# Feed-forward passes over one column tile: 1024 inner channels at a time instead of 512

## The chip, the core and the metric

The kernel runs on one core of a Trainium2 chip. Five engines of the core work side by side and meet through semaphores: TensorE (PE in the profile, its weight loads PEld), VectorE (DVE), ScalarE (ACT), GpSimd (POOL) and SyncE (SP), which here issues nearly all DMAs. The metric is the device time of one execution, in microseconds (us). One profiled execution gives the trace; its times are the ones quoted, counted from the start of the span.

## The reference

Two layers of a streaming encoder are run for 1024 prompt frames and 32 sample frames that share all weights, in float32. Layer 0 mixes with a spatial gating unit, layer 1 with a pooling mixer; each is followed by the feed-forward network (FFN) that the change is about. Cut to that part:

```python
D_MODEL = 1024; D_FF = 4 * D_MODEL
for i in range(2):
    mod = silu(c) @ w_ada[i] + b_ada[i]              # 6 conditioning vectors of 1024
    sh1, sc1, gt1, sh2, sc2, gt2 = split(mod, 6)
    ...                                              # mixer, residual with gt1
    h = rmsnorm(x, g_norm[i, 2]) * (1 + sc2) + sh2
    f = square(relu(h @ ffn_w_up[i])) @ ffn_w_down[i]
    x = x + gt2 * rmsnorm(f, g_norm[i, 3])
```

`c` is one vector per group, so the prompt frames share one set of conditioning vectors and the sample frames another. The matrices are 1024 by 4096 up and 4096 by 1024 down.

## The kernel before

**Layout.** Activations lie transposed: 128 channels on the partitions, frames along the free axis, 8 blocks of 128 channels (`KB`). The 1056 frames form three column tiles (`TILES`): 384, 384, and 256 prompt + 32 sample frames = 288. `acc[t]` holds a tile's accumulator, `hh[t]` and `hl[t]` the normalised input as a high and a low part. Every float32 product is made of three matmuls in the rounded format `F32R` (`products`, lines 1024 to 1026 of the profile): high weight by high input, high by low, low by high.

**Weights.** A weight piece of 512 KB is loaded into one of three staging buffers (`raw`, `RAW_SLOTS`), copied to its high part by ScalarE (line 528) and subtracted to its low part by VectorE (`wl`). High and low part take two of 16 slots (`w_tile`); four slots are lent out and called back once the FFN starts (`LEND_AT`, `w_call`), so the FFN holds at most six pieces. `stream` is the one list in which all pieces are loaded, with pieces of `w_ada` between them (`some_ada`); the latter are multiplied and summed on VectorE (`aa`, four instructions a piece, a fold after every fourth).

**FFN passes.** `passes` lists the FFN's work in order: (layer, 512-channel block, tiles). For one tile, `ffn_item` makes four up products of 24 matmuls (`up(j)`; ScalarE applies relu, square and the high copy `fh`, VectorE the low part `fl`) and puts the down products into `pending`. They are issued by `flush()` behind the first up product of the next pass, so the last `fl` has that long to get ready. `down()` makes eight products of 12 matmuls (`pg`), each with an addition to `acc` on VectorE (`accumulate`; the first block is a copy on ScalarE). For the first two tiles together, `pair_item` needs seven block products where two tiles would need eight, from input combinations made by `combos()`; its down products follow at once. The hidden parts live in five places each (`t_hid`); the pair borrows staging tiles for three more.

**Order.** The program is written out by Python. `fillers` are generators with the vector work between matrix products: `ffn0_t` (after the gating mixer: residual, norm, modulation, which `ffn0`'s first pass on tile t needs), `ffn1_t` (residual of layer 0's FFN, pooling mixer, residual, norm, modulation for layer 1), `out_t` (the output). `weave()` runs after every product: it takes at most one piece of the stream, and then steps of the first two fillers as long as a planner's clock for VectorE is behind its clock for TensorE. An addition is booked at 0.16 us + n/930, other operations alike; a filler may ask for a gap (`yield 1.2`), in which the second filler is served. Where a pass begins a tile, `finish()` issues the rest of its filler at once (`run_ffn`). The framework then puts each engine's instructions in its own queue; instructions that are ready can be moved ahead of others there, and `PE` mostly stays in written order.

The pair combinations use the memory of the lent slots (tag `R`); `singles` tells `combos()` that it may start.

Of the kernel before, what the change touches and what calls it, by code (L numbers as in the profile page):

```python
# [10 lines left out]
F32R = mybir.dt.float32r  # L11
# [4 lines left out]
P = 128  # L16
# [11 lines left out]
NT = len(TILES)  # L28
# [7 lines left out]
def tile_stream_encoder_step(  # L36
# [100 lines left out]
    def ps_up(name):  # L137
        return psum.tile([P, 512], F32, tag="pu", bufs=2, name=name)
# [7 lines left out]
    def t_m(name):  # L146
        return work.tile([P, 384], F32, tag="m", bufs=3, name=name)
# [4 lines left out]
    def t_hid(kind, name, dtype=F32R):  # L152
        return work.tile([P, 384], dtype, tag="h" + kind, bufs=5, name=name)
# [88 lines left out]
    def add_w(key, ap, shape, kind="w"):  # L242
        stream.append((kind, key, ap, shape))
# [21 lines left out]
    lent = {"left": LENT, "called": False}  # L265
# [18 lines left out]
    def w_free(key):  # L284
        for i in held.pop(key):
            if i >= 0 and lent["called"]:
                lent["left"] -= 1
            else:
                slots.append(i)
# [60 lines left out]
                )  # L350

    def w_chunk(n):
        l, c, tiles = passes[n]
        for j in range(4):
            f = 4 * c + j
            add_w(
                ("up", n, j),
                ffn_w_up[l][:, f * P : (f + 1) * P].rearrange("(k p) f -> p k f", p=P),
                (8, P),
                ("one", "two")[j % 2] if tiles == PAIR else "w",  # L360
            )
        for q in range(4):
            add_w(
                ("dn", n, q),
                ffn_w_down[l][c * 512 : (c + 1) * 512, q * 256 : (q + 1) * 256].rearrange(
                    "(j p) d -> p j d", p=P
                ),
                (4, 256),
            )

    every = list(range(NT))
    PAIR = every[:2]
    passes = [(0, c, [0]) for c in (0, 1, 6, 7)]
    passes += [(0, c, [1]) for c in (0, 1)]
    passes += [(0, c, PAIR) for c in range(2, 6)]
    passes += [(0, c, [1]) for c in (6, 7)]
    passes += [(0, c, [NT - 1]) for c in range(8)]
    passes += [(1, c, [t]) for t in PAIR for c in range(4)]  # L380
    passes += [(1, c, PAIR) for c in range(4, 8)]
    passes += [(1, c, [NT - 1]) for c in range(8)]
    LEND_AT = ("up", 0, 0)

    rest = []
# [1 line left out]
    def some_ada(n):  # L387
        for _ in range(min(n, len(rest))):
            add, l, j = rest.pop(0)
            add(l, j)  # L390
# [25 lines left out]
    for n in range(len(mixes)):  # L416
        w_groups(n)
        if n < 2:
            some_ada(8)
    for n, (l, c, tiles) in enumerate(passes):  # L420
        w_chunk(n)
        if tiles == PAIR:
            some_ada((6, 2)[l])
        elif l == 0 and c > 1 and len(tiles) == 1 and tiles != [NT - 1]:
            some_ada(2)
    some_ada(99)

    worder = [s[1] for s in stream if s[0] in ("w", "one", "two")]
# [236 lines left out]
    def run_deferred(force=False):  # L665
        n = len(deferred)
        while n > 0 and (force or deferred[0][0] <= time["pe"]):
            deferred.pop(0)[1]()
            n -= 1
# [31 lines left out]
    def stream_ready():  # L701
        k = state["next"]
        if k >= len(stream):
            return False
        if subs:
            return len(slots) >= subs[0][0]
        return len(slots) >= {"w": 2, "one": 3, "two": 3}.get(stream[k][0], 0)

    def stream_step():

        if not subs and stream[state["next"]][0] == "one":
            issue()
            state["next"] += 1
        k = state["next"]
        kind, key, ap, shape = stream[k]
        issue()
        run_deferred()
        if kind == "two":
            if not subs:
                quads(key[1], key[2], raws.pop(k - 1), raws.pop(k))  # L720
            subs.popleft()[1]()
            if not subs:
                state["next"] += 1
            issue()
            return
        r = raws.pop(k)
        if kind == "w":
            do_w(key, r)
        elif kind == "wide":
            do_ada(*key, r, 512)  # L730
        elif kind == "ada":
            if k < first_ada:
                do_ada_pe(*key, r)
            else:
                do_ada(*key, r, 256)
        else:
# [27 lines left out]
    def w_finish(key):  # L764
        w_free(key)
# [511 lines left out]
    pending = []  # L1277
# [43 lines left out]
    def sgu_item(p, t, mix, after):  # L1321
# [123 lines left out]
                flush()  # L1445
        pending.append(down)

    def ffn_item(p, t, after):
        l, c, tiles = passes[p]
        last = t == tiles[-1]  # L1450
        n = ncol[t]
        hid = []

        def up(j):
            ps = ps_up(f"pf{l}_{c}_{t}_{j}")
            products(ps, n, up_terms(("up", p, j), t))
            if last:
                w_finish(("up", p, j))
            r = t_m(f"r{l}_{c}_{t}_{j}")
            act(out=r[:, :n], in_=ps[:, :n], func=AF.Relu)  # L1460
            a, b = t_hid("h", f"fh{l}_{c}_{t}_{j}"), t_hid("l", f"fl{l}_{c}_{t}_{j}")
            act(out=r[:, :n], in_=r[:, :n], func=AF.Square)
            split(a, b, r, n)
            hid.append((a, b))

        def down():
            for d in range(KB):
                ps = ps_dn(f"pg{l}_{c}_{t}_{d}")
                wh, wl = need_w(("dn", p, d // 2))
                terms = []  # L1470
                for j in range(4):
                    o = j * 256 + (d % 2) * P
                    a, b = hid[j]
                    terms.append((wh[:, o : o + P], wl[:, o : o + P], a[:, :n], b[:, :n]))
                products(ps, n, terms)
                accumulate(t, d, ps, c == 0)
                if d == 0 and after is not None:
                    st = Stat(t, f"rf{l}_{t}", l == 0 or t < NT - 1)
                if after is not None:
                    st.square(d)  # L1480
                    if l == 1 and t == NT - 1:
                        scale_last(d)
                        if d < len(LAST):
                            turn_x(d)
                        if d in (2, 4, 6):
                            turn_last(d - 2)
                            turn_last(d - 1)
                if last and d % 2 == 1:
                    w_finish(("dn", p, d // 2))
                weave(d % 2)  # L1490
            if after is not None:
                after(st)

        for j in range(4):
            up(j)
            weave()
            if j == 0:
                flush()
                if l == 1 and c == 7 and last and t == NT - 1:
                    load_last()  # L1500
        pending.append(down)


    def pair_item(p, after, ends):
        l, c, tiles = passes[p]
        n = ncol[0]
        hid = {t: [None] * 4 for t in tiles}
        made = [0]
# [181 lines left out]
    singles = []  # L1690
# [208 lines left out]
        fillers.append((f"ffn1_{t}", run()))  # L1899

    def run_ffn(l, after):
        for p, (pl, c, tiles) in enumerate(passes):
            if pl != l:
                continue
            ends = [t for t in tiles if not any(q[0] == l and t in q[2] for q in passes[p + 1 :])]
            if tiles == PAIR:
                pair_item(p, after, ends)
                continue
            for t in tiles:
                if c == 0:  # L1910
                    if any(f[0] == f"ffn{l}_{t}" for f in fillers):
                        flush()
                    finish(f"ffn{l}_{t}")
                if tiles == [1] and c == 0:
                    singles.append(l)
                ffn_item(p, t, after if t in ends else None)

    run_ffn(0, to_pool)


# [154 lines left out]
```

## Time and profile before

| | us |
|---|---|
| median of 3 runs (2162.13 to 2167.15) | 2162.45 |
| the profiled execution | 2162.36 |
| its span, first to last instruction | 2160.6 |
| PE busy | 2116.0 (98%) |
| DVE busy | 1580.9 (73%) |
| ACT busy | 1050.2 (49%) |
| mean busy share of the 16 DMA engines, queue q1 | 48.2% |

The profiled execution takes 1.8 us beyond its span and lies 0.1 us under the median. Matmuls overlap, so a row gives one of 384 columns some 0.33 us while the next starts 0.17 us later; the number of matmuls that start in a stretch tells more than PE's busy time. The FFN of layer 0 runs from 613 to 1385 us, that of layer 1 from 1391 to 2151 us. Of each, the passes are: first tile alone, second tile alone, pairs, (layer 0: second tile again,) third tile.

### The profile page before, as it was taken

The numbers are of one execution on the slowest core, as the hardware profiler recorded it, in microseconds if no ns is written. First come the engines' busy times: TensorE is split into PE (matmuls) and PEld (weight loads), VectorE is DVE, ScalarE is ACT, GpSimd is POOL, SyncE is SP. The second block draws the span as 40 slices with busy tenths as digits, with TensorE's granted clock in tenths as the row PEclk, the third lists the DMA queues.
The fourth block names the chain that finished last, engine by engine and source line by source line (L and its number), as shares of the span: only waits on it lengthen the run. The fifth ranks groups of instructions, "written<-read, shape, count | busy, mean of one in ns | idle before, by whom it ended". The sixth has DMA issues, their size and how long they took to land.

```text
span 2160.6 us, 33037 instructions
## 1 busy us (share of the span) xinstructions
PE 2116.0 (98%) x12930; PEld 2045.1 (95%) x12930; DVE 1580.9 (73%) x2778; ACT 1050.2 (49%) x1801; POOL 22.3 (1%) x44
## 2 busy tenths in 40 slices
PE   8999999999999999999999999799999999999998
PEld 6878999999999999999998999799999999999998
DVE  6778837567788757788886896957969765588564
ACT  5634331233455454443455666555655443455454
POOL 0000000000000000000000000000000000001100
PEclk9999999999999999999999999899999999999999
DMA  8586524353344543333474765455544322247762
GB/s 289 167 257 209 183 76 135 99 161 114 115 135 126 162 126 99 116 117 108 138 225 137 214 201 180 135 154 164 167 139 127 108 81 85 80 129 224 176 187 82
DMA packets 401904, 320.16 MB, mean 148 GB/s; under 512 B 47406, under 2 KB 365142, under 8 KB 401748
## 3 DMA queue, kind: packets, MB, share of 16 engines
q1 hardware_dynamic: 400820, 316.77, 48.2%
q8 instruction: 101, 1.65, 0.3%
q0 software_dynamic: 896, 1.28, 0.2%
q14 instruction: 55, 0.45, 0.1%
q10 hardware_dynamic: 32, 0.01, 0.0%
HBM read 287.34 MB, written 30.66 MB: 147 GB/s over the span
## 4 chain that ended last, share of the span: by engine, by line
PE 86%; DVE 6%; DMA 3%; ACT 3%; issue 1%; DVEq 0%; SPq 0%; ACTq 0%
PE pg L1025 10%; PE pg L1026 10%; PE pg L1024 10%; PE pf L1024 7%; PE pf L1025 7%; PE pf L1026 7%; PE po L1024 3%; PE po L1025 3%; PE po L1026 3%; PE pu L1024 3%; PE pu L1026 3%; PE pu L1025 3%; DMA raw<-in_w_ada_dram 2%; PE pv L1050 2%; PE pv L1052 2%; PE pv L1051 2%
## 5 line engine op out<-in xcount | busy, mean ns | idle before, releaser
L1024 PE MATMUL pg<-fh,wh_dn 128*128 128x384 f32 (+1 forms) x1344 | 431.5, 322 | 2.4 <-ACT wh_dn L528 2.4
L1026 PE MATMUL pg<-fh,wl_dn 128*128 128x384 f32 (+1 forms) x1344 | 429.1, 319 | 0.4 <-DVE wl_dn L80 0.4
L1025 PE MATMUL pg<-fl,wh_dn 128*128 128x384 f32 (+1 forms) x1344 | 429.3, 320 | 0.2 <-DVE fl L80 0.2
L1024 PE MATMUL pf<-hh,wh_up 128*128 128x384 f32 (+1 forms) x1024 | 325.6, 319 | 11.2 <-ACT hh L984 6.5
L1025 PE MATMUL pf<-hl,wh_up 128*128 128x384 f32 (+1 forms) x1024 | 324.4, 317 | 0.0
L1026 PE MATMUL pf<-hh,wl_up 128*128 128x384 f32 (+1 forms) x1024 | 323.7, 316 | 0.3 <-DVE wl_up L80 0.2
L528 ACT ACTIVATE wh_dn<-raw 128x1024 fp32r<-128x1024 f32 x160 | 169.1, 1058 | 198.6 <-PE pg L1025 126.8
L1024 PEld LDWEIGHTS pg<-fh,wh_dn 128*128 128x128 f32 x1344 | 252.5, 188 | 4.2 <-ACT wh_dn L528 2.6
L80 DVE TENSOR_TENSOR wl_dn<-raw,wh_dn 128x1024 fp32r<-128x1024 f32 x160 | 195.7, 1224 | 83.0 <-ACT wh_dn L528 76.6
L1025 PEld LDWEIGHTS pg<-fl,wh_dn 128*128 128x128 f32 x1344 | 252.7, 188 | 1.6 <-DVE fl L80 0.7
L1026 PEld LDWEIGHTS pg<-fh,wl_dn 128*128 128x128 f32 x1344 | 252.9, 188 | 0.7 <-DVE wl_dn L80 0.7
L80 DVE TENSOR_TENSOR acc<-acc,pg 128x384 f32<-128x384 f32 (+1 forms) x336 | 173.4, 518 | 72.9 <-PE pg L1026 72.6
L80 DVE SCALAR_TENSOR_TENSOR aa<-raw,csil,aa 128x512 f32<-128x512 f32 (+1 forms) x364 | 206.7, 623 | 20.9 <-DMA raw<-in_w_ada_dram 20.9
L80 DVE TENSOR_TENSOR wl_up<-raw,wh_up 128x1024 fp32r<-128x1024 f32 x128 | 156.3, 1222 | 81.7 <-ACT wh_up L528 81.5
L1024 PEld LDWEIGHTS pf<-hh,wh_up 128*128 128x128 f32 x1024 | 193.7, 190 | 14.0 <-ACT hh L984 7.6
L528 ACT ACTIVATE wh_up<-raw 128x1024 fp32r<-128x1024 f32 x128 | 135.5, 1060 | 130.0 <-PE pf L1025 78.4
L1026 PEld LDWEIGHTS pf<-hh,wl_up 128*128 128x128 f32 x1024 | 194.3, 190 | 1.0 <-DVE wl_up L80 0.9
L1025 PEld LDWEIGHTS pf<-hl,wh_up 128*128 128x128 f32 x1024 | 194.1, 190 | 0.9 <-DVE hl L80 0.7
L80 DVE TENSOR_TENSOR fl<-r,fh 128x384 fp32r<-128x384 f32 (+1 forms) x168 | 87.0, 519 | 43.1 <-ACT fh L1284 42.0
L1024 PE MATMUL po<-ush,wh_o 128*128 128x384 f32 (+1 forms) x336 | 108.0, 321 | 0.0
L1026 PE MATMUL po<-ush,wl_o 128*128 128x384 f32 (+1 forms) x336 | 107.7, 321 | 0.0
L1025 PE MATMUL po<-usl,wh_o 128*128 128x384 f32 (+1 forms) x336 | 107.7, 320 | 0.0
(387 smaller groups left out, 4254.7 us busy)
## 6 DMA issues: line engine op xcount, KB each, us to landing
raw<-in_ffn_w_up_dram SPq DMA_DIRECT2D x160, 512.0 KB, 4.0
raw<-in_ffn_w_down_dram SPq DMA_DIRECT2D x160, 512.0 KB, 3.4
raw<-in_w_ada_dram SPq DMA_DIRECT2D x92, 512.0 KB, 4.3
raw<-in_sgu_w_in_dram SPq DMA_DIRECT2D x40, 512.0 KB, 4.0
xd<-acc SPq DMA_DIRECT2D x8, 1536.0 KB, 7.8
raw<-in_sgu_w_out_dram SPq DMA_DIRECT2D x24, 512.0 KB, 3.6
xo_r<-xd SPq DMA_DIRECT2D x32, 384.0 KB, 4.0
vd<-vt SPq DMA_DIRECT2D x32, 256.0 KB, 4.5
```

Of the source, the lines that this page charges most:

```text
L80: return op(out, *args, **kw)
L528: act(out=wh, in_=r, func=AF.Copy)
L1024: mm(ps[:, :n], wh, rh, start=i == 0, stop=False)
L1025: mm(ps[:, :n], wh, rl, start=False, stop=False)
L1026: mm(ps[:, :n], wl, rh, start=False, stop=i == last)
L1050: mm(ps[:m, :], a_h, wh[:, o : o + 512], start=k == 0, stop=False)
L1051: mm(ps[:m, :], a_h, wl[:, o : o + 512], start=False, stop=False)
L1052: mm(ps[:m, :], a_l, wh[:, o : o + 512], start=False, stop=k == KB - 1)
```

## The change

The tuple of a pass gets a fourth member m, the number of 512-channel blocks that it takes. For m = 2 there are eight up products and then eight down products of 24 matmuls, each over eight hidden blocks, with one addition to the accumulator where there were two. A down piece of the weights is then 1024 channels by 128 columns instead of 512 by 256. The down products of such a pass aren't put into `pending` but issued directly behind its last up product. Thirteen passes have m = 2: two of the first tile, one of the second and four of the third in layer 0, two and four of the first and third in layer 1. Passes of the second tile before the pairs, and the pairs, stay as they are; in layer 0 the pairs take blocks 4 to 7 instead of 2 to 5. The eight `w_ada` pieces that were spread two by two behind four single passes of layer 0 stand four by four behind the two passes of the first tile. The hidden parts of m = 2 use five more places, in memory of tag `R`; so `singles` is set later, after the first up product on the second tile.

```diff
 def w_chunk(n):
-        for j in range(4):
+        for j in range(4 * m):
...
-        for q in range(4):
+        w = 256 // m
+        for q in range(4 * m):
             add_w(
                 ("dn", n, q),
-                ffn_w_down[l][c * 512 : (c + 1) * 512, q * 256 : (q + 1) * 256].rearrange(
+                ffn_w_down[l][c * 512 : (c + m) * 512, q * w : (q + 1) * w].rearrange(
                     "(j p) d -> p j d", p=P
                 ),
-                (4, 256),
+                (4 * m, w),
...
-    passes = [(0, c, [0]) for c in (0, 1, 6, 7)]
-    passes += [(0, c, [1]) for c in (0, 1)]
-    passes += [(0, c, PAIR) for c in range(2, 6)]
-    passes += [(0, c, [1]) for c in (6, 7)]
-    passes += [(0, c, [NT - 1]) for c in range(8)]
-    passes += [(1, c, [t]) for t in PAIR for c in range(4)]
-    passes += [(1, c, PAIR) for c in range(4, 8)]
-    passes += [(1, c, [NT - 1]) for c in range(8)]
+    passes = [(0, c, [0], 2) for c in (0, 2)]
+    passes += [(0, c, [1], 1) for c in (0, 1)]
+    passes += [(0, c, PAIR, 1) for c in range(4, 8)]
+    passes += [(0, 2, [1], 2)]
+    passes += [(0, c, [NT - 1], 2) for c in (0, 2, 4, 6)]
+    passes += [(1, c, [0], 2) for c in (0, 2)]
+    passes += [(1, c, [1], 1) for c in range(4)]
+    passes += [(1, c, PAIR, 1) for c in range(4, 8)]
+    passes += [(1, c, [NT - 1], 2) for c in (0, 2, 4, 6)]
...
         if tiles == PAIR:
             some_ada((6, 2)[l])
-        elif l == 0 and c > 1 and len(tiles) == 1 and tiles != [NT - 1]:
-            some_ada(2)
+        elif l == 0 and tiles == [0]:
+            some_ada(4)
...
+    more_hid = [None, 0]
+
+    def take_hid(name, many):
+
+        if not many:
+            more_hid[:] = [None, 0]
+        else:
+            i = more_hid[1]
+            more_hid[1] += 1
+            if i % 10 >= 5:
+                if more_hid[0] is None:
+                    assert not lent["left"]
+                    more_hid[0] = work.tile([P, 5, 2, 384], F32R, tag="R", bufs=1, name="fx" + name)
+                return more_hid[0][:, i % 5, 0], more_hid[0][:, i % 5, 1]
+        return t_hid("h", "fh" + name), t_hid("l", "fl" + name)
...
 def ffn_item(p, t, after):
-            a, b = t_hid("h", f"fh{l}_{c}_{t}_{j}"), t_hid("l", f"fl{l}_{c}_{t}_{j}")
+            a, b = take_hid(f"{l}_{c}_{t}_{j}", m > 1)
...
-                wh, wl = need_w(("dn", p, d // 2))
+                wh, wl = need_w(("dn", p, d * m // 2))
                 terms = []
-                for j in range(4):
-                    o = j * 256 + (d % 2) * P
+                for j in range(4 * m):
+                    o = j * 256 // m + (d % 2) * P * (2 - m)
...
-                weave(d % 2)
+                weave((d + 1) * m % 2 == 0)
...
-        for j in range(4):
+        for j in range(4 * m):
             up(j)
             weave()
             if j == 0:
                 flush()
+                if tiles == [1] and c == 0:
+                    singles.append(l)
...
-        pending.append(down)
+        if m > 1:
+            down()
+        else:
+            pending.append(down)
```

More of the change, by code (lines that the diff above doesn't have):

```diff
@@ L352, in w_chunk @@
     def w_chunk(n):
-        l, c, tiles = passes[n]
-        for j in range(4):
+        l, c, tiles, m = passes[n]
+        for j in range(4 * m):
             f = 4 * c + j
@@ L419, in tile_stream_encoder_step @@
             some_ada(8)
-    for n, (l, c, tiles) in enumerate(passes):
+    for n, (l, c, tiles, m) in enumerate(passes):
         w_chunk(n)
@@ L1446, in sgu_item @@
         pending.append(down)
+    more_hid = [None, 0]
[11 more added lines that the diff above has]
+        return t_hid("h", "fh" + name), t_hid("l", "fl" + name)
     def ffn_item(p, t, after):
-        l, c, tiles = passes[p]
+        l, c, tiles, m = passes[p]
         last = t == tiles[-1]
@@ L1487, in down @@
                             turn_last(d - 1)
-                if last and d % 2 == 1:
-                    w_finish(("dn", p, d // 2))
-                weave(d % 2)
+                if last and (d + 1) * m % 2 == 0:
+                    w_finish(("dn", p, d * m // 2))
+                weave((d + 1) * m % 2 == 0)
             if after is not None:
                 after(st)
-        for j in range(4):
+        for j in range(4 * m):
             up(j)
@@ L1498, in ffn_item @@
                 flush()
-                if l == 1 and c == 7 and last and t == NT - 1:
+                if tiles == [1] and c == 0:
+                    singles.append(l)
+                if l == 1 and c + m == 8 and last and t == NT - 1:
                     load_last()
-        pending.append(down)
+        if m > 1:
+            down()
+        else:
+            pending.append(down)
     def pair_item(p, after, ends):
-        l, c, tiles = passes[p]
+        l, c, tiles, _ = passes[p]
         n = ncol[0]
@@ L1901, in run_ffn @@
     def run_ffn(l, after):
-        for p, (pl, c, tiles) in enumerate(passes):
+        for p, (pl, c, tiles, m) in enumerate(passes):
             if pl != l:
@@ L1913, in run_ffn @@
                     finish(f"ffn{l}_{t}")
-                if tiles == [1] and c == 0:
-                    singles.append(l)
                 ffn_item(p, t, after if t in ends else None)
```

## The prediction

> **What bounds the kernel.** I read the page first, then the table of waits for TensorE, then its busy time stretch by stretch.
>
> ```profile
> span 2160.6 us, 33037 instructions
> ...
> PE 2116.0 (98%) x12930; PEld 2045.1 (95%) x12930; DVE 1580.9 (73%) x2778; ACT 1050.2 (49%) x1801; POOL 22.3 (1%) x44
> ```
>
> TensorE is the bound, and the change takes no matmul away: two passes of 192 become one of 384. What can be won is only the time in which TensorE stands. The additions that go are VectorE's, 73% busy on average. Where does TensorE stand, and on whom?
>
> ```profile
> PE pn_r_0x L897 <- ACT sc_r_0x L882: 8.8, 1, 8.8
> PE pf L1024 <- ACT hh L984: 6.5, 2, 5.1
> ...
> PE pf L1024 <- ACT wh_up L528: 3.7, 2, 2.0
> PE pn_rf L897 <- ACT sc_rf L882: 2.7, 1, 2.7
> PE pg L1024 <- ACT wh_dn L528: 2.4, 1, 2.4
> PE pg L1025 <- DVE fx L80: 1.8, 6, 0.5
> ```
>
> Total, times, longest: a few long waits. The stretches around them, with two undisturbed ones first (core, PE busy with its count, PEld, DVE, ACT, POOL, clock, DMA):
>
> ```profile
> 1116.00:1134.00 18.00, 18.00 (x106) 18.00 (x105) 14.79 (x22) 8.24 (x12) 0.00 (x0) 1.00 0.47 139
> 2060.00:2078.00 18.00, 18.00 (x138) 18.00 (x137) 13.38 (x16) 8.77 (x12) 0.00 (x0) 1.00 0.69 204
> 1094.00:1104.00 10.00, 8.22 (x47) 7.76 (x46) 8.92 (x13) 4.58 (x8) 0.00 (x0) 1.00 1.02 298
> 1146.00:1170.00 24.00, 18.91 (x113) 17.09 (x106) 19.40 (x51) 14.79 (x35) 0.00 (x0) 0.86 0.24 70
> 1372.00:1396.00 24.00, 10.13 (x49) 8.78 (x48) 23.71 (x39) 10.33 (x18) 0.00 (x0) 0.64 0.45 143
> 2042.00:2060.00 18.00, 15.24 (x103) 14.67 (x102) 6.33 (x10) 7.80 (x13) 0.00 (x0) 0.91 0.54 153
> 2078.00:2090.00 12.00, 10.03 (x64) 9.80 (x63) 6.10 (x7) 6.43 (x12) 0.00 (x0) 0.86 0.80 230
> ```
>
> A matmul of 384 columns takes 18/106 = 0.17 us, one of 288 18/138 = 0.13. What a stretch lacks beyond its own matmuls is lost, the low clock included:
> - D, 1094 to 1104: 10 - 47 x 0.17 = 2.0 us; a weight's load is late.
> - A, 1146 to 1170, the third tile of layer 0 begins: some 28 of 384 columns and 85 of 288, so 24 - 4.8 - 11.1 = 8.1 us.
> - B, 1372 to 1396, layer 1 begins: 32 of 288 and 17 of 384, so 24 - 4.2 - 2.9 = 16.9 us. VectorE is busy for 23.7 of these 24.
> - C, 2042 to 2060 and 2078 to 2090: 18 - 103 x 0.13 = 4.6 and 12 - 64 x 0.13 = 3.7, together 8.3 us.
>
> 35.3 us in all can be won at these four places.
>
> **The change, part by part.** Additions: a double pass issues 8 where two single passes issued 16, so each of the 13 double passes saves 8, 104 in all.
>
> ```profile
> L80 DVE TENSOR_TENSOR acc<-acc,pg 128x384 f32<-128x384 f32 x224 | 123.2, 551 | 48.4 <-PE pg L1026 48.2
> L80 DVE TENSOR_TENSOR acc<-acc,pg 128x288 f32<-128x288 f32 x112 | 50.2, 451 | 24.5 <-PE pg L1026 24.4
> ```
>
> Directly they are worth nothing: they run beside 12 other matmuls. They count where VectorE's queue of filler steps is late for a boundary, A and B.
>
> At A, the norm of the third tile is late. VectorE's groups from 1080 to 1146:
>
> ```profile
> L80 DVE SCALAR_TENSOR_TENSOR aa<-raw,csil,aa 128x512 f32<-128x512 f32 x14 | 9.8, 748 | 0.0
> L80 DVE TENSOR_TENSOR acc<-acc,pg 128x384 f32<-128x384 f32 x16 | 8.8, 552 | 7.5 <-PE pg L1026 7.5
> L80 DVE STREAM_TRANSPOSE raw<-aa 128x512 f32<-128x512 f32 x2 | 1.3, 688 | 0.0
> L630 DVE TENSOR_REDUCE part<-raw 128x16 f32<-128x512 f32 x2 | 1.3, 678 | 0.0
> ...
> L80 DVE TENSOR_SCALAR aa<-raw,csil 128x512 f32<-128x512 f32 x2 | 0.9, 483 | 0.0
> ```
>
> Four conditioning pieces (`aa`, 13.3 us with their folds) move 350 us earlier, half the 16 additions go (4.4): 17.7 us. Still to do behind the boundary was the modulation:
>
> ```profile
> 1155.31 1.21 DVE L80 SCALAR_TENSOR_TENSOR acc<-acc,coef,r_r_2x 128x256 f32<-128x256 f32 x4
> ```
>
> eight such rows, 9.7 us. That fits into 17.7, so I take 7.5 of A's 8.1 as gone. D goes with the `w_ada` loads ahead of the late weight: 1.5 of 2.0.
>
> At B the first tile's filler (residual, pooling, residual, norm) is late. VectorE is free of 17.7 us up to A and of 32 x 0.451 = 14.4 in the third tile's passes, 32 us in all; the planner, whose books charge 0.16 + 288/930 = 0.47 for the addition, gives the same to fillers. What VectorE still had to do for the first tile after 1377 is some 15 us: two scalings, sums and squares (6), then 16 steps of modulation:
>
> ```profile
> 1390.40 1.67 DVE L80 SCALAR_TENSOR_TENSOR acc<-acc,coef,r_r_0x 128x384 f32<-128x384 f32 x3
> ```
>
> at 0.53 each, 8.5 us. So even if the second filler takes half of the 32, B shrinks to little: 14 of 16.9, 3 kept for a rest. If the stall goes, next late is the second tile's filler at 1530, where nothing stood before.
>
> At C the weights come too late. SyncE's queue:
>
> ```profile
> 2029.03 13.13 SPq L1941 DMA_DIRECT2D out_dram<-y_sq  x23
> 2042.25 1.52 SPq L476 DMA_DIRECT2D raw<-in_ffn_w_down_dram  x3
> ```
>
> 23 output stores stand between two weight loads for 13.1 us. Six pieces are held, each good for 24 x 0.13 = 3.1 us, and three may be staged. Before, the next pass's first up piece is used ahead of four down pieces that were loaded before it, so five of six places are needed for one product and the next piece gets its place one product ahead. With down products at once, pieces are used in loading order, and the full 6 x 3.1 = 18.7 us plus staging (9.4) stand against 13.1 + 4 (landing) + 2.3 (both halves): C goes, 6 of 8.3 taken, since when the stores are issued moves too.
>
> The start of the down products is the price: the eighth hidden block is needed after 21 matmuls, where it used to have an up product more. The only such start now is the last pass (ScalarE's queue, VectorE's and TensorE's):
>
> ```profile
> 2136.34 0.41 ACT L1460 ACTIVATE r<-pf 128x288 f32<-128x288 f32 x1 [1.84 <-PE pf L1026]
> 2137.26 0.45 ACT L1284 ACTIVATE fh<-r 128x288 fp32r<-128x288 f32 x1
> 2137.73 0.46 DVE L80 TENSOR_TENSOR fl<-r,fh 128x288 fp32r<-128x288 f32 x1 [2.74 <-ACT fh L1284]
> ...
> 2136.14 0.30 PE L1024 MATMUL pg<-fh,wh_dn 128*128 128x288 f32 x1
> ```
>
> The down product starts at 2136.14, `fl` is there at 2138.19: 2.05 us, 3.1 with a weight's copy (1.06) ahead. Cover is 22 x 0.13 = 2.9 us on the third tile, 3.7 on the others: a wait of 0 to 0.2. Above, the pairs, which start likewise with only nine matmuls, wait 1.8 us in six places, 0.3 each. I take 0.2, nearest to the last pass: 13 x 0.2 = 2.6; bounds 0 and 13 x 0.3 = 3.9. Were the five new places one unit to the waits, the sixth block would wait for the eighth: 15 x 0.13 = 1.95 us of cover, up to 1.1 more each; matmuls that read single slices of `acc` and `hh` beside writers of others speak against that.
>
> The rest has one answer. New places: double passes write a place only behind the matmuls that read it, no wait. `combos` can't use tag `R` before 744 (it ran from 643):
>
> ```profile
> 642.89 0.95 DVE L80 TENSOR_TENSOR combo_x<-hh,hl 128x768 f32<-128x768 f32 x1
> 744.00:829.00 85.00, 84.81 (x490) 84.50 (x489) 51.00 (x68) 40.75 (x65) 0.00 (x0) 1.00 0.39 118
> ```
>
> some 12 us of it move into 85 us in which VectorE idles 34. The eight conditioning pieces ahead (13.3 us more, 16 x 0.55 = 8.8 us of additions less) lie in the first tile's 133 us; four in a row hold the weights up by 13 us, less than six pieces (25 us at 0.17): 0.5 for both. Down pieces with runs of 512 bytes, not 1024:
>
> ```profile
> raw<-in_ffn_w_up_dram SPq DMA_DIRECT2D x160, 512.0 KB, 4.0
> raw<-in_ffn_w_down_dram SPq DMA_DIRECT2D x160, 512.0 KB, 3.4
> ```
>
> Up pieces have such runs already and land 0.6 us later: 104 x 0.6 = 62 us of landing, all behind three staged pieces, 0 on the path; without that cover C would stay. [...]
>
> Sum: 1.5 + 7.5 + 14 + 6 = 29.0 gained, 2.6 + 0.5 = 3.1 paid, net 25.9. The profiled execution took 2162.4 us (span and 1.8), a tenth under the median: 2136.5.
>
> **The rivals.** First: the second filler eats what is freed, B stays. For it: while the first filler sits out its gaps, the second is served. Against it: the gaps are few, and 32 us stand against 15. Time: 2162.4 - 15.0 + 3.1 = 2150.5.
>
> Second: the waits at A and B aren't VectorE's backlog but the chain of the norm itself (sum, root, first modulation), which comes at each boundary, and C only shifts with the stores. For it: the longest wait at A ends on `sc`, the norm's factor, and not on an addition or a copy. Against it: VectorE is busy for 23.7 of 24 us at B. Then only D goes: 2162.4 - 1.5 + 3.1 = 2164, no change.
>
> Third, slower: every double pass waits at its down start, because `fl` stands behind filler steps in VectorE's queue. It has happened:
>
> ```profile
> 1094.33 2.74 DVE L80 SCALAR_TENSOR_TENSOR aa<-raw,csil,aa 128x512 f32<-128x512 f32 x4
> 1096.98 0.56 DVE L80 TENSOR_TENSOR fl<-r,fh 128x384 fp32r<-128x384 f32 x1
> ```
>
> With 2.7 us ahead of it in each of 13 passes, `fl` is 2.8 us late: 36 us, 2162.4 - 29 + 36 + 0.5 = 2170. It decides from (29 - 0.5 + 6.5)/13 = 2.7 us a pass on. Against it: half of the passes have little filler work, and the pairs lose 0.3. [...]
>
> **Chances.** Forecast, with A, B, C mostly gone (2124 to 2146): 0.58. Second filler: 0.17. No change: 0.12. Slower: 0.13. Faster by over 0.3% (6.5 us, about what a measurement tells from none) is 0.75, within it 0.12, slower 0.13. The range runs from all four places won, no price, and a few us of smaller waits (2162.4 - 35.3 - 5 = 2122) to the middle of the second rival, 2162.
>
> **What will show it.** A: no `pn_rf` wait and full clock as the third tile begins. B: the wait of 8.8 us gone, `hh` of layer 1 written before the last down product ends. C: no waits for `wh` after the stores. Price: waits of `pg` on `fh` or `fl` at 13 starts, 0.2 us each. Wrong if `pn_r_0x` still waits over 5 us, if `pg` waits come to over 10 us, or if waits for `wh` appear among the first tile's passes.

## The result, and the profile after

The changed kernel takes 2128.6 us (median of four runs, 2127.77 to 2130.07), the kernel before 2162.6 on the same chip: a ratio of 0.9839, with a 95% interval of 0.9822 to 0.9856. That is 34 us less. The profiled execution took 2129.34 us, its span is 33.0 us shorter than the span before.

The head of the page, and its row of engines:

```profile
span 2127.6 us, 32971 instructions
PE 2106.0 (99%) x12930; PEld 2040.5 (96%) x12930; DVE 1537.8 (72%) x2674; ACT 1048.7 (49%) x1801; POOL 22.3 (1%) x44
```

TensorE issues as many matmuls as before (12930), VectorE 104 operations less. So the 33 us are time in which TensorE stood or ran at a low clock. The waits of TensorE (total, times, longest), and its busy time in the stretches that answer to those of the prediction (D; A; B in two rows; C; and five microseconds out of C):

```profile
PE pf L1024 <- ACT wh_up L528: 2.4, 1, 2.4
...
PE pf L1026 <- DVE wl_up L80: 0.7, 1, 0.7
PE pg L1024 <- ACT fh L1284: 0.6, 1, 0.6
```

```profile
1080.00:1114.00 34.00, 34.00 (x196) 33.76 (x196) 22.38 (x33) 22.93 (x37) 0.00 (x0) 1.00 0.81 254
1147.00:1173.00 26.00, 26.00 (x196) 26.00 (x195) 19.77 (x27) 19.16 (x35) 0.00 (x0) 1.00 0.75 222
1338.00:1364.00 26.00, 26.00 (x198) 25.91 (x197) 17.21 (x26) 12.16 (x19) 0.00 (x0) 1.00 0.66 195
1364.00:1380.00 16.00, 16.00 (x88) 14.94 (x87) 7.85 (x10) 10.46 (x18) 0.00 (x0) 1.00 0.49 137
2007.00:2038.00 31.00, 27.88 (x197) 27.41 (x196) 17.21 (x19) 17.56 (x30) 0.00 (x0) 0.94 0.54 153
2008.00:2013.00 5.00, 3.23 (x25) 3.00 (x23) 0.79 (x2) 1.67 (x4) 0.00 (x0) 1.00 0.00 0
```

The waits of 8.8, 6.5 and 2.7 us on the norm's parts are gone, and as the third tile (1147) and layer 1 (1364) begin, TensorE is busy all the time at full clock. Of the four places C is what is left: the three waits above, between 2011 and 2043.

The table below holds the time lost at these places in every trace that bears on it. For each run of like matmuls in a trace, its length less its count times 0.1733 us (384 columns) or 0.1333 us (288) was taken, and these remainders were added over the place, the pooling's products left out: D from the last pair pass of layer 0 to the third tile's start, A the 55 us around that start, B from there to 33 us into layer 1, C the third tile's passes of layer 1. It is the prediction's rule; over 48 like matmuls in a row, the median pace is 0.1733 us in both traces for 384 columns, and for 288 it is 0.1327 in that of before and 0.1333 in that of the changed kernel. Some tenths of an entry may be matmuls whose records are missing. In a second trace of the changed kernel (`after_again`) D loses 0.6 us more and C 0.5 less, so differences of that size between two rows say nothing.

| us lost | D | A | B | C |
|---|---|---|---|---|
| before | 3.2 | 8.5 | 18.8 | 8.0 |
| changed kernel | 0.4 | 0 | 1.9 | 5.8 |
| adds_back | 1.1 | 0.6 | 2.2 | 4.6 |
| adds_unplanned | 0.2 | 0.9 | 4.2 | 5.7 |
| before_early | 1.4 | 1.2 | 3.1 | 7.1 |
| late_ada2 | 1.4 | 6.8 | 2.7 | 5.4 |
| dummy_ada | 0.1 | 8.4 | 3.2 | 4.3 |
| late_ada | 1.6 | 9.7 | 21.4 | 2.6 |
| before_now | 7.6 | 3.2 | 17.1 | 8.2 |
| before_order | 0.6 | 2.2 | 13.7 | 6.5 |
| stores_spread | 0.1 | 0 | 3.1 | 11.8 |
| stores_pool_again | 0.2 | 0 | 2.2 | 0 |

Of the 33 us, D, A, B and C hold 38.5 - 8.1 = 30.4.

### The profile page after: what moved, and what is told of

Its sections match the earlier page's. It is cut to its first block, busy times and chain, and to the rows that moved or that the text cites. A ratio compares the mean times of both kernels' runs of the same rounds, so it can differ in the third digit from the quotient of the medians.

```text
span 2127.6 us, 32971 instructions
## 1 busy us (share of the span) xinstructions
PE 2106.0 (99%) x12930; PEld 2040.5 (96%) x12930; DVE 1537.8 (72%) x2674; ACT 1048.7 (49%) x1801; POOL 22.3 (1%) x44
## 4 chain that ended last, share of the span: by engine, by line
PE 92%; DVE 3%; DMA 2%; ACT 1%; issue 1%; SPq 0%; DVEq 0%; ACTq 0%
PE pg L1025 11%; PE pg L1026 11%; PE pg L1024 11%; PE pf L1024 7%; PE pf L1026 7%; PE pf L1025 7%; PE pu L1024 3%; PE pu L1026 3%; PE pu L1025 3%; PE po L1024 3%; PE po L1025 3%; PE po L1026 3%; PE pv L1050 2%; PE pv L1052 2%; PE pv L1051 2%; DMA raw<-in_w_ada_dram 2%
## 5 line engine op out<-in xcount | busy, mean ns | idle before, releaser
L1024 PE MATMUL pg<-fh,wh_dn 128*128 128x384 f32 (+1 forms) x968 | 314.3, 325 | 0.7 <-ACT fh L1284 0.6
L1025 PE MATMUL pg<-fl,wh_dn 128*128 128x384 f32 (+1 forms) x968 | 313.4, 324 | 0.1
L1026 PE MATMUL pg<-fh,wl_dn 128*128 128x384 f32 (+1 forms) x968 | 313.1, 323 | 0.0
L80 DVE TENSOR_TENSOR acc<-acc,pg 128x384 f32<-128x384 f32 (+1 forms) x232 | 122.4, 528 | 98.2 <-PE pg L1026 98.2
L1024 PEld LDWEIGHTS pg<-fh,wh_dn 128*128 128x128 f32 x968 | 181.7, 188 | 1.4 <-ACT fh L1284 1.1
L1025 PE MATMUL pg<-fx,wh_dn 128*128 128x384 f32 (+1 forms) x568 | 181.0, 319 | 1.9 <-DVE fx L80 1.8
L1025 PEld LDWEIGHTS pg<-fl,wh_dn 128*128 128x128 f32 x968 | 181.7, 188 | 0.5 <-DVE fl L80 0.3
L1024 PE MATMUL pg<-fx,wh_dn 128*128 128x384 f32 (+1 forms) x568 | 181.4, 319 | 0.3 <-ACT fx L1284 0.3
L1026 PEld LDWEIGHTS pg<-fh,wl_dn 128*128 128x128 f32 x968 | 181.7, 188 | 0.0
L1026 PE MATMUL pg<-fx,wl_dn 128*128 128x384 f32 (+1 forms) x568 | 179.7, 316 | 0.0
L1025 PEld LDWEIGHTS pg<-fx,wh_dn 128*128 128x128 f32 x568 | 106.6, 188 | 4.7 <-DVE fx L80 3.8
```

The lines of the kernel that those rows point to most:

```text
L80: return op(out, *args, **kw)
L1024: mm(ps[:, :n], wh, rh, start=i == 0, stop=False)
L1025: mm(ps[:, :n], wh, rl, start=False, stop=False)
L1026: mm(ps[:, :n], wl, rh, start=False, stop=i == last)
```

## The experiments

The theory to be tested: A and B are filler work of VectorE that is late, and the change frees time for it in two ways, by conditioning pieces that go earlier and by additions that go away; C is a matter of the loading order. The rivals: one of the two ways did it all; or neither, and the new order of the products did it.

Each kernel was timed side by side with the kernel before, which took 2166.9, 2166.1 or 2164.8 us there (medians). So the ratios are to be compared, not the times, and a gain in us is a ratio taken of 2162.6. A forced step, in the expectations, is a filler step that `finish()` has to issue at a boundary.

**Which part cured A and B.** Five kernels take the parts one by one. `before_early` is the kernel before with the pieces moved and nothing else:

```
-        elif l == 0 and c > 1 and len(tiles) == 1 and tiles != [NT - 1]:
+        elif l == 0 and tiles == [0]:
             some_ada(2)
```

> The kernel before, with all eight conditioning pieces behind the first tile's four passes, nothing else. Theory: D goes (2 us), A shrinks from 9 to 3 us (five forced steps instead of eleven), B from 17 to 5 to 9 us: 2162.6 - 16 to - 20 = 2143 to 2147. Rival (only the pieces matter): D, A and B gone, 2134. Rival (order or additions alone): 2160 to 2163.

Measured: 2138.9 us, 0.9877 of before (0.9862 to 0.9891). The pieces alone bring some 27 us, more than expected.

`late_ada2` is the other half: the change without the move of the pieces. Its four late pieces stand behind one double pass, where the kernel before has two behind each of two single passes. A first attempt, `late_ada`, took the condition without the list of tiles, so four further pieces, which belong far behind, came to stand in the third tile's passes.

```
-        elif l == 0 and tiles == [0]:
+        elif l == 0 and c == 2 and tiles in ([0], [1]):      # late_ada2
+        elif l == 0 and len(tiles) == 1 and m > 1 and c == 2:  # late_ada
             some_ada(4)
```

> The changed kernel, with four of the eight conditioning pieces behind the late double pass of tile 1 again, as they were, so that their 13.3 us of VectorE lie between 1046 and 1114. Theory: A comes back by a little (two forced steps, 0 to 3 us), B by 6 to 12 us (twelve forced steps), D by 0 to 2: 2136 to 2145. Rival (only the pieces matter): all of A, B and D is back, 2128.6 + 28 = 2156. Rival (only the order matters): 2129.

> The changed kernel with four conditioning pieces behind the first tile's second double pass and four behind the second tile's late double pass, as many as in the kernel before at either place. (The run late_ada put four more behind the third tile's second double pass, which was not meant: its 27 us are not the price of the move alone.) Theory (VectorE's time before the two boundaries counts, whichever part of the change frees it; the books leave one forced step at A and three at B): 2130 to 2137. Rival (the place of the pieces is what cured A and B, the eight-block passes nothing): 2148 to 2156, with the waits of the kernel before at 1150 and 1385.

Measured: `late_ada` 2155.8 us, 0.9954 (0.9937 to 0.9970); `late_ada2` 2141.8 us, 0.9889 (0.9874 to 0.9904). The eight-block passes without the move bring 24 us, less than the theory and more than the rival said. The same stretches in the two (of `late_ada2` A in two rows and the end of layer 0; of `late_ada` a stretch in the third tile's passes and the start of layer 1):

```profile
1149.00:1180.00 31.00, 29.57 (x218) 28.17 (x217) 27.54 (x39) 23.03 (x38) 0.00 (x0) 1.00 0.77 220
1180.00:1210.00 30.00, 28.12 (x198) 27.66 (x199) 15.69 (x17) 14.05 (x22) 0.00 (x0) 0.94 0.76 225
1346.00:1374.00 28.00, 26.74 (x201) 26.28 (x200) 26.68 (x44) 18.27 (x32) 0.00 (x0) 1.00 0.56 159
```

```profile
1262.00:1310.00 48.00, 43.89 (x312) 42.84 (x312) 41.36 (x55) 29.90 (x46) 0.00 (x0) 0.96 0.90 276
1382.00:1405.00 23.00, 13.74 (x57) 12.22 (x56) 21.61 (x35) 11.53 (x21) 0.00 (x0) 0.70 0.30 85
```

So at B either way does without the other: with the additions back but the pieces early, B is 3.1 us, with the pieces late but the additions gone (and the products in their new order), 2.7, and before it was 18.8. Each alone is enough, and 24 + 27 us are more than the 34 that both give. In `late_ada` four more pieces ahead of layer 1 bring B back (57 matmuls in 23 us, clock 0.70), though the additions are gone.

A has to be read by its waits. The third tile's norm (`r_2x`, its sum `pn_r_2x`) is what the prediction found late there. TensorE takes up its sum in the kernel before and in `late_ada2` at

```profile
1150.30 0.29 PE L897 MATMUL pn_r_2x<-sc_r_2x,ones 128*128 128x288 f32 x1
```

```profile
1114.76 0.29 PE L897 MATMUL pn_r_2x<-sc_r_2x,ones 128*128 128x288 f32 x1
```

In `late_ada2` the norm isn't late. What it loses at A, 6.8 us, are waits of another kind, on hidden blocks and on a weight's low part (the longest between 1140 and 1190):

```profile
PE pg L1024 <- ACT fx L1284: 1.4, 1, 1.4
PE pf L1026 <- DVE wl_up L80: 0.8, 1, 0.8
PE pg L1025 <- DVE fl L80: 0.5, 1, 0.5
```

The late pieces' work on VectorE (16 `aa` operations) lies behind the norm there, between 1118 and 1160, beside the third tile's first pass; in the kernel before all of it lay ahead of the norm's sum, between 1091 and 1130. So `late_ada2` doesn't tell which part of the change moved the norm.

`adds_back` puts 104 operations of VectorE into the changed kernel, `adds_unplanned` the same ones past the planner's books (0.16 us and a part by columns for each operation, by which the planner sets where each filler step stands in the program):

```
                 accumulate(t, d, ps, c == 0)
+                if m > 1:
+                    x = acc[t][:, d, HALO:HALO + n]
+                    tt(out=x, in0=x, in1=x, op=ALU.max)  # adds_back
+                    nc.vector.tensor_tensor(out=x, ...)  # adds_unplanned
```

> The changed kernel, with 104 VectorE operations put back: behind every addition or copy of a double pass one more operation over the same slice of acc, which leaves it as it is, charged to the planner's books as the additions were. Theory (A and B are VectorE's backlog, and the additions were over half of what B needed): B comes back in part, A hardly, since the books leave two forced steps there and eighteen at the start of layer 1: 8 to 15 us of standing TensorE at B, 0 to 2 at A, 2138 to 2146. Rival (the order of the work, down products at once and weights in order of use, is what cured A and B): no stall, 2129 to 2132. Rival (the conditioning pieces alone cured them): 2129 to 2132 too.

> The same 104 VectorE operations in the changed kernel, but the planner's books don't know of them, so that every filler step keeps its place in the order. Theory (VectorE's queue itself is late): the first tile's filler ends some 30 us ahead of layer 1 in the books and some 20 us of operations are put ahead of it, so B stays away; A has 4 us of room for 4 us: 0 to 4; together 2129 to 2135. If filler order doesn't matter and only VectorE's load does: the same as with the books charged, 2138 to 2146.

Measured: 2134.8 us, 0.9857 (0.9842 to 0.9871), and 2137.7 us, 0.9870 (0.9856 to 0.9885), beside 0.9839 and, in a second measurement below, 0.9850 for the changed kernel. The first can't be told from it, the second lies 0.2 to 0.3% above it, with intervals that meet, and above the 2129 to 2135 of its theory. Neither brings A or B back, against what the theory expected of `adds_back`. What they cost is spread over the passes.

`dummy_ada` puts 13.2 us of VectorE, without any load, among the up products of the second tile's late double pass, ahead of the norm:

```
             up(j)
+            if l == 0 and c == 2 and t == 1:
+                for d in range(3):
+                    x = acc[t][:, 4 * (j % 2) + d, HALO:HALO + n]
+                    tt(out=x, in0=x, in1=x, op=ALU.max)
             weave()
```

> The changed kernel with 24 more VectorE operations of 0.55 us (acc with itself, maximum, which leaves it as it is) among the up products of the second tile's late double pass: 13.2 us of VectorE at the place from which the four conditioning pieces went, without their loads. Theory (A is VectorE's backlog and nothing else): 13 us against 4 us of room; the third tile's norm is late again by 5 to 9 us, B by 0 to 3 us more: 2136 to 2142. Rival (the loads in the staging places made A and D): 2128 to 2130.

Measured: 2140.9 us, 0.9885 (0.9870 to 0.9899). A is back with 8.4 us, and on the norm: TensorE waits 2.0 us for `hh`, its result. So the norm's place hangs on VectorE's time ahead of it, as the planner counts it. D is not back (0.1 us). In the kernel before D's wait ends on a load; ScalarE's queue:

```profile
1098.75 1.06 ACT L528 ACTIVATE wh_up<-raw 128x1024 fp32r<-128x1024 f32 x1 [3.88 <-DMA raw<-in_ffn_w_up_dram]
```

That load was issued at 1093.32, behind two `w_ada` loads from 1086.10 on. But no run puts these loads back alone: the 1.4 us of `late_ada2` are no wait on a weight, and `before_early`, with the pieces early, has 1.4 too. That the `w_ada` loads make D is read from this trace and not shown by a run.

Is VectorE truly full ahead of A? Its queue, TensorE's, and a stretch of both in `dummy_ada` (in brackets the idle time before an instruction and who ended it):

```profile
1114.35 0.52 DVE L80 SCALAR_TENSOR_TENSOR sm_r_2x<-sq_r_2x,eps,sc_r_2x 128x288 fp32r<-128x288 f32 x1
...
1118.06 0.55 DVE L80 TENSOR_TENSOR acc<-acc,pg 128x384 f32<-128x384 f32 x1 [1.19 <-PE pg L1026]
...
1122.22 0.56 DVE L80 TENSOR_TENSOR acc<-acc,pg 128x384 f32<-128x384 f32 x1 [2.02 <-PE pg L1026]
...
1143.02 0.55 DVE L80 TENSOR_TENSOR acc<-acc,pg 128x384 f32<-128x384 f32 x1 [1.55 <-PE pg L1026]
...
1145.60 0.45 DVE L80 SCALAR_TENSOR_TENSOR q_r_2x<-pn_r_2x,q_r_2x 128x288 f32<-128x288 f32 x1
```

```profile
1142.82 0.29 PE L897 MATMUL pn_r_2x<-sc_r_2x,ones 128*128 128x288 f32 x1
...
1149.76 0.53 PE L1024 MATMUL pf<-hh,wh_up 128*128 128x288 f32 x2 [1.99 <-ACT hh L984]
```

```profile
1114.00:1143.00 29.00, 29.00 (x170) 29.00 (x169) 15.59 (x21) 11.16 (x17) 0.00 (x0) 1.00 0.51 148
```

No. The sum's input `sm_r_2x` is there at 1114.87, TensorE takes it up at 1142.82, the next step on VectorE follows at 1145.60, and in between VectorE is busy for 15.6 of 29 us; it waits 1.2 to 2.0 us ahead of the additions shown. The norm stands behind the additions because it was put there. The kernel before looks the same ahead of A and of B:

```profile
1114.00:1150.00 36.00, 35.84 (x212) 35.02 (x211) 28.21 (x45) 15.95 (x24) 0.00 (x0) 1.00 0.51 152
...
1303.00:1363.00 60.00, 59.89 (x405) 55.37 (x404) 42.91 (x67) 39.88 (x70) 0.00 (x0) 1.00 0.54 166
```

VectorE idles 7.8 of 36 us and 17.1 of 60, and then is busy behind the boundary (19.4 of 24 us at A, 23.7 of 24 at B) with steps that had been put there. So what the change frees seems to be booked time first of all: with it the planner puts the steps ahead of the boundary. That the books charge too much is read from the code and these rows; a run with `dummy_ada`'s operations past the books, which would tell book from queue at this place, was not made.

**The order of the products and of the loads.** `before_now` issues the down products of each single-tile pass at once, in the kernel before; `before_order` keeps the products' order and loads the next pass's first up piece ahead of the down pieces:

```
-        pending.append(down)
+        down()                                  # before_now, ffn_item
```

```
-        for j in range(4):                      # before_order, w_chunk
-            f = 4 * c + j
+        ahead = n + 1 < len(passes) and tiles != PAIR and passes[n + 1][2] != PAIR
+        begun = n > 0 and tiles != PAIR and passes[n - 1][2] != PAIR
+        ups = [(n, j) for j in range(begun, 4)] + ([(n + 1, 0)] if ahead else [])
+        for m, j in ups:
+            f = 4 * passes[m][1] + j
             add_w(
-                ("up", n, j),
+                ("up", m, j),
...
```

> The kernel before, with the down products of every single-tile pass directly behind its own up products (nothing held over to the next pass), nothing else; weights are then used in loading order. Theory: C goes (6 to 8 us); each of 26 single-tile passes now starts its down products after nine matmuls of cover and waits 0.2 to 0.4 us (5 to 10 us); A and B shrink a little (by the books five and fourteen forced steps for eleven and eighteen), 4 to 8 us: 2154 to 2160. Rival (order alone is the cause): A, B, C and D gone, 35 less and 5 to 10 for the starts: 2133 to 2138.

> The kernel before, with the first up piece of the next single-tile pass loaded ahead of the four down pieces, in the order in which they are used; the order of the products stays. Theory: C goes, 6 to 8 us, and D with it (2): 2152 to 2155; if the planner's books are right on A and B (three and eleven forced steps), they shrink by up to 11 us more, 2142. If C isn't the loading order: no change but A and B, 2151 to 2162.

Measured: `before_now` 2163.6 us, 0.9986 (0.9976 to 0.9996); `before_order` 2146.0, 0.9906 (0.9890 to 0.9922). The first hardly differs from the kernel before, the second is some 20 us faster. Both use their weights in loading order, and both still lose 6.5 us and more in C. Of `before_order` the start of layer 1 and C, of `before_now` D and C:

```profile
1365.00:1395.00 30.00, 22.61 (x120) 20.93 (x119) 28.98 (x46) 15.94 (x29) 0.00 (x0) 0.83 0.29 85
2029.00:2050.00 21.00, 17.88 (x112) 17.41 (x111) 7.06 (x10) 8.65 (x16) 0.00 (x0) 0.84 0.61 171
```

```profile
1099.00:1123.00 24.00, 20.14 (x99) 19.65 (x98) 14.99 (x21) 7.64 (x10) 0.00 (x0) 0.86 0.63 196
...
2043.00:2075.00 32.00, 29.61 (x201) 29.09 (x200) 14.83 (x21) 12.28 (x19) 0.00 (x0) 0.89 0.56 154
```

C is two waits on weights in the kernel before, 2.4 us on `wh_dn` at 2054 and 2.0 us on `wh_up` at 2084. `before_early`, with the old loading order, keeps both (2.4 and 1.5 us). The two kernels here keep the first at 2.4 us and are rid of the second, in whose place they wait for hidden blocks (1.0 and 0.4 us). So the loading order makes the second wait and not the first.

That down products at once cured B falls: with them alone B keeps 17.1 us. A is 3.2 us with them. `before_order` gains 20 us, by A (6.3), B (5.1) and D (2.6) more than by C (1.5): the order of the loads shifts the filler steps as well. TensorE takes up the third tile's norm at 1114.64 in it, 36 us earlier than in the kernel before, though VectorE has the same pieces and additions to work on; half of the pieces' work has come to lie behind the norm, between 1130 and 1142. So the same work in another order is enough at A. Of several things in the change that can cure A's norm, the runs don't say which did.

**C.** In the changed kernel, SyncE's queue, ScalarE's and TensorE's around 2011:

```profile
1985.30 14.17 SPq L1960 DMA_DIRECT2D out_dram<-y_sq  x24
1999.57 2.94 SPq L476 DMA_DIRECT2D raw<-in_ffn_w_up_dram  x3
```

```profile
2011.27 0.41 ACT L1476 ACTIVATE r<-pf 128x288 f32<-128x288 f32 x1 [18.05 <-PE pf L1026]
...
2012.54 2.94 ACT L528 ACTIVATE wh_up<-raw 128x1024 fp32r<-128x1024 f32 x3
```

```profile
2013.63 0.40 PE L1024 MATMUL pf<-hh,wh_up 128*128 128x288 f32 x1 [2.40 <-ACT wh_up L528]
```

24 stores still stand between two weight loads for 14.2 us. But the pieces issued by 2002.5 have landed when TensorE wants them: from 2008 to 2013 the DMA engines do nothing (their share is 0.00 in the last row of the stretches above). ScalarE has been idle for 18 us, with the copies of the weights in its queue: they stand behind the `r` of the pass's first hidden block, which TensorE has yet to finish. C's first wait in the kernel before looks the same (ScalarE's queue, and a stretch of all engines):

```profile
2051.68 0.41 ACT L1460 ACTIVATE r<-pf 128x288 f32<-128x288 f32 x1 [1.83 <-PE pf L1026]
...
2052.95 2.94 ACT L528 ACTIVATE wh_dn<-raw 128x1024 fp32r<-128x1024 f32 x3
```

```profile
2049.50:2053.00 3.50, 2.15 (x17) 1.91 (x15) 0.46 (x1) 1.60 (x5) 0.00 (x0) 1.00 0.01 2
```

The three pieces issued from 2042.25 on have landed, the DMA engines are idle, and the copies come behind an `r`. Its second wait is another: that piece was issued at 2077.65 and copied at 2082.66, as soon as it had landed.

Two runs on the stores. In `stores_spread` they go in six steps of four; in `stores_pool` the second tile's go to GpSimd's queue:

```
-                store_out(1, nc.sync, range(6))
-                store_out(1, nc.gpsimd, range(6, KB))
+                store_out(1, nc.gpsimd, range(KB))     # stores_pool
+                for k in range(6):                     # stores_spread
+                    store_out(1, nc.sync, [k])         #   (the last two ks stay on gpsimd)
+                    yield 2.0
```

> The changed kernel, with the second tile's stores on SyncE's queue as before, but in six steps of four, each of them let in by the planner at least 2 us after the one before. Theory: weight loads get between them, the wait at 2011 goes: 2122.5 to 2125. Rival (ScalarE's order): 2128 to 2129.

> The changed kernel, with the second tile's output stores all issued on GpSimd's queue and none of them on SyncE's. Theory (C is what is left of the stores that stand between weight loads): the wait on wh_up at 2011 and the low clock behind it go, 5 to 6 us: 2122.5 to 2124. Rival (the pieces had long landed and ScalarE's order, conversions behind the relu of the first block, makes the wait): 2128 to 2129.

Measured: `stores_spread` 2139.9 us, 0.9876 (0.9861 to 0.9892), slower than the changed kernel's 0.9839 (the interval meets that of its second measurement below), C 11.8 us. Now each of six loads has four stores ahead of it, and copies still stand behind an `r`: a piece issued at 2011.83 is copied at 2023.30, though the DMA engines' share is 0.00 from 2017 to 2020. `stores_pool` took 2127.3 us, 0.9816 (0.9801 to 0.9832). C is gone in its trace, but it lost 5.9 us at one pair pass's down products, where the changed kernel lost 1.1 and the two programs are the same. So both were run once more, side by side:

> The changed kernel once more, beside the next one: 2128 to 2130, with some 6 us lost between 2005 and 2065 (C).

> The changed kernel with the second tile's stores all on GpSimd's queue, once more, with more rounds: C's 6 us are gone in the trace of its first run, but 4.8 us more were lost behind the down products of one pair pass near 1744, where the two programs are the same. If that was this one execution: 2123 to 2125, 4 to 6 us under the changed kernel. If it comes with the change: 2127.

Measured: 2133.0 us, 0.9850 (0.9834 to 0.9866), and 2125.8, 0.9815 (0.9800 to 0.9830): 7.2 us less, intervals apart. This is the fastest kernel of the study. The pair pass lost 1.7 us this time. The third tile's passes in `after_again` and in `stores_pool_again`, and ScalarE's queue in the latter:

```profile
2000.00:2060.00 60.00, 56.67 (x411) 55.84 (x411) 30.87 (x37) 27.34 (x42) 0.07 (x1) 0.97 0.68 183
```

```profile
2000.00:2060.00 60.00, 60.00 (x455) 59.90 (x454) 34.86 (x41) 29.95 (x44) 14.65 (x24) 1.00 0.73 200
```

```profile
2009.71 1.06 ACT L528 ACTIVATE wh_up<-raw 128x1024 fp32r<-128x1024 f32 x1 [2.10 <-DVE acc L80]
2012.34 0.41 ACT L1476 ACTIVATE r<-pf 128x288 f32<-128x288 f32 x1 [1.57 <-PE pf L1026]
```

With the stores away, the copies also stand ahead of `r` in ScalarE's queue. The order of a queue belongs to the program: ScalarE's 1801 instructions come in one order in both traces of the changed kernel, and in another, which differs in 29 places around C, in both traces of `stores_pool`. That it follows from times assumed for the loads, the stores among them, is an inference. Whether the old order alone, with the stores away, would still cost C was not tried. Moved to GpSimd, 24 stores take 14.65 us of its time (POOL in the second stretch above); on SyncE's queue 24 took 14.17.

## Why the prediction was right, point by point

It forecast 2136.5 us and faster with 0.75; measured were 2128.6 in the run with the prediction's own pair, 7.9 less. By its steps, against the profiled executions:

- **D**, 1.5 taken: 2.8 gained. The trace of before fits the reason given, a load behind the `w_ada` loads, and 24 operations without loads leave D away; no run puts the loads back alone.
- **A**, 7.5 taken: 8.5 gained. Its longest wait, 2.7 us on `sc_rf`, is for a norm over 384 columns, an FFN output's, and not for the third tile's (288). The size came out, the reason only in part, so the hit is partly luck. The additions aren't needed: with them put back A loses 0.6. Nor is the time that the prediction counted as freed, 17.7 us against 9.7: in `before_order`, which takes no work away and moves no conditioning piece, the norm comes at 1114.64, in the changed kernel at 1113.40, and A loses 2.2. "Late" was not "VectorE has no time". The prediction looked at the 24 us behind the boundary (VectorE busy 19.4) and not at the 36 us ahead of it, in which VectorE idles 7.8.
- **B**, 14 taken: 16.9 gained. Here 32 freed us were set against 15, and that either half would be enough was not seen. The measured sums show it: 24 and 27 us apart, 34 together.
- **C**, 6 taken: 2.2 gained. This step failed. "With down products at once, pieces are used in loading order ... C goes" holds for the second of C's two waits alone, the one on a piece that landed late. The first has stayed, at 2.4 us: it is a copy's place in ScalarE's queue, with the piece landed. The rows that would have said so stood in the trace of before, where the copies of `wh_dn` come behind an `r` and the DMA share is 0.01.
- **Price of the down start**, 2.6 paid: none. The rows at the start of the second tile's double pass show why (ScalarE's, VectorE's and TensorE's queues):

```profile
1114.39 0.48 ACT L1476 ACTIVATE r<-pf 128x384 f32<-128x384 f32 x1
1115.80 0.53 ACT L1284 ACTIVATE fx<-r 128x384 fp32r<-128x384 f32 x1
1116.36 0.56 DVE L80 TENSOR_TENSOR fx<-r,fx 128x384 fp32r<-128x384 f32 x1
...
1114.02 0.34 PE L1024 MATMUL pg<-fh,wh_dn 128*128 128x384 f32 x1
...
1117.83 0.33 PE L1025 MATMUL pg<-fx,wh_dn 128*128 128x384 f32 x1
```

  The eighth block is there at 1116.92 and wanted at 1117.83, 0.9 us later. The lower bound of 0, which followed from 2.05 us against 2.9 to 3.7, was the right one; the 0.3 us of the pairs was no neighbour, since they have nine matmuls of cover, not 21. The one wait of this kind (0.6 us on `fh`) is in C.
- **The rest**, 0.5 paid: 33.0 - 30.4 = 2.6 gained over the other stretches, of which 1.8 in layer 1's passes before the pairs; their parts were not followed up. The down pieces land in a median of 4.0 us now, 3.4 before; the 62 us counted for that were hidden, as said: the longest waits on weights are the 2.4 and 0.7 us of C.

The sum, 25.9, is short by 7.1: B 2.9, D 1.3 and A 1.0 more, no price (2.6), the rest 3.1, against C's 3.8 less.

Of the rivals, the first (the second filler takes what is freed) did not happen even with the additions put back. The second (the norm's chain itself) is out: the chain is unchanged and A and B are gone. The third's mechanism exists: in `late_ada2` TensorE waits 1.4 us for a hidden block's `fx` as the third tile's first down products begin, and most of its loss at A is of this kind. But in the changed kernel no such wait is left outside C.

## What to carry to other kernels

A stall at a boundary whose work stands in an engine's queue says nothing on whether that engine is full: look at the same engine ahead of the boundary, and if it idles there (VectorE here for 7.8 of 36 us), look for who fixed the order. Two reliefs of one wait need not add up (24 and 27 us here, 34 together); each of them undone alone tells which place needs which, if the waits are read and not only the time lost: a place can lose as much as before on another wait. A transfer that seems late may have landed: a DMA share of 0.00, as here from 2008 to 2013, beside a wait on a copy of a weight sends the eye to the queue that copies.

## What the runs showed of the hardware

In two places short waits cost more than their length. In C the waits on weights are 2.4 and 0.7 us and the stretch loses 5.1; the granted clock is 0.80 from 2013 to 2016 and 0.63 from 2016 to 2019. In the first run of `stores_pool` waits of 0.4, 1.4 and 0.2 us within 3 us at one pair pass came to 5.9 lost. There too the granted clock tells why (that pass in two rows):

```profile
1744.00:1750.00 6.00, 3.95 (x13) 2.90 (x12) 6.00 (x13) 5.37 (x11) 0.00 (x0) 0.74 0.30 87
1750.00:1756.00 6.00, 6.00 (x26) 6.00 (x26) 4.59 (x9) 0.00 (x0) 0.00 (x0) 0.69 0.31 87
```

In the second row TensorE is busy all of 6 us and does 26 matmuls where 34 fit; from 1747 to 1753 the granted clock is 0.50. It fell after some 2 us of waits with matmuls between them, and came back some 7 us later. In another execution of the same program the waits there were 0.6 and 0.5 us, the clock stayed at 1.00, and 1.7 us were lost.
